# A scratch round trip in a planned stream of instructions: the read back as a step of its own, and a plan that no longer counts the turning

## The chip, the core and the metric

The kernel runs on one core of a Trainium2 chip. The core has five engines that each work through their own list of instructions in order: TensorE (PE, with its weight loads shown as PEld), VectorE (DVE), ScalarE (ACT), GpSimd (POOL) and SyncE (SP). SP issues nearly all DMAs of this kernel, and since its list is in order too, an issue that waits holds back all that stand behind it. The engines wait for each other through semaphores. The metric is the device time of one execution in microseconds; the number that counts is the median of several runs.

## What is computed

One inference step of a trunk of two layers over 512 prompt tokens and 32 sample tokens, with 1024 features. Layer 0 mixes tokens with RWKV-7 time mixing, layer 1 with differential attention; both also attend to a memory of 256 tokens, gate the result and project it back:

```
def rwkv_layer(x, mk, mv, prev_row, S0, ...):
    h = rmsnorm(x, norm_w)
    p, qm, gate = split(h @ w_in)
    y_mix, S_T, last_row = rwkv_mixer(p, prev_row, S0, ...)
    y_mem = mem_attention(qm, mk, mv)
    out = concatenate([y_mix, y_mem]) * silu(gate)
    return x + out @ w_out, S_T, last_row

def step(S, inp):                      # inside rwkv_mixer, for every token and each of 24 heads
    r_t, k_t, v_t, w_t, kk_t, a_t = inp
    sa = einsum('bhvk,bhk->bhv', S, -kk_t)
    S = S * w_t + sa * (kk_t * a_t) + v_t * k_t
    return S, einsum('bhvk,bhk->bhv', S, r_t)
```

Everything is in float32. The change is in layer 0.

## The kernel before

**Blocks.** The projections `h @ w_in` go block by block: one block is 128 columns of the weight, that is 1024 x 128 numbers. They are loaded as two halves (tile `raw`, `load`, L264, five buffers). Each half is split for TensorE into a rounded part `whi` (a cast on ScalarE) and the rest `wlo` (a subtraction on VectorE) (`split`, L293), and a block then takes 48 products into two PSUM tiles `ps_g` (`steps`, L348). In layer 0 these products are the filling between all else, and the list of TensorE is laid out so that it always has some.

**Pairs.** The 24 heads are done as 12 pairs. The recurrence over tokens is cut into chunks of 64. A pair's *preparation* (`rw_prep`, L645) makes decays, keys and the small matrices of each chunk; it is a Python generator, and each `yield` ends a step. It has 33 steps. Near its end it needs the keys turned round, tokens on partitions. VectorE's transpose turns blocks of 32 x 32 only (two instructions from `bk` into `bt`); the blocks themselves are put in their places by a round trip through scratch memory in DRAM:

- step 30: the two transposes, and four DMAs from `bt` to the scratch `tscr`;
- steps 31 and 32: the values are turned on TensorE and copied to `sv`;
- step 33: one DMA of 512 KB from `tscr` back to the whole tile `bt`.

A DMA that reads what another wrote waits, on its issuing queue, until those have landed. `bt` and `tscr` have two buffers each. The pair's *chain* (`chunk`, L957) multiplies by a slice of `bt` in each of its chunks.

**Other steps around it.** A pair's triangular matrices go to scratch (`sc1`, step 26 of the preparation), are inverted on GpSimd (`inv`, L851), and come back in two steps (`back`, L875, and `at`, L885). `val`, `mrg`, `smp`, `out` and `fin` are further generators of a pair. `go(kind, pr)` (L1476) calls the next step of one of them.

**The order.** For layer 0 the order on every engine and queue is the order in which the program issues (`tie`, L123). First come three lists: `FILL0`, `FILL1` and `FILL2` (L83 on) call a step of the preparation of pair 0, 1 and 2, each followed by so many products of the blocks (loops at L1587, L1595, L1610). After that each pair's chain runs in 23 steps, numbered from 0, by `PLAN` (L49). Each step has two halves, and each half lists what is called there: a kind, the distance of its pair from the pair of the chain, its cost on TensorE's side and its cost on VectorE, both in us. The products are handed out so that TensorE's costs are spread evenly. Products, casts and subtractions all come from one stream (L1557), which asks for the load of a block two blocks ahead.

**Work put off.** The casts and subtractions of the next block, and some other evacuations, are put off into a queue (`put_off`, L305). Each half step calls `some(room)` (L315), with

```
room = (sum(load) + 2.3 * each[pr] / 48) / len(PLAN)
spent += self.some(room * (k + (half + 1) / 2) + 0.4 - spent)
```

where `load` holds the VectorE costs of the steps, `each` the products of the pair, and `spent` what VectorE has been booked for so far in the pair. A subtraction has the cost `LATER` (0.75) and is issued only when the allowance is at least that; casts cost nothing and go at once. What is still in the queue when its block begins is issued there (`until`, L310).

**The end of pair 9.** Pairs are numbered from 0. When the chain of pair 9 is through (`pr + 3 == NPAIR`), the last steps of the preparation of pair 11 are called, with the 24 products that were kept back (`KEPT`). Then its pool of tiles is closed, and the pool of the memory attention takes its place. That attention begins with loads of the cached memory keys (`cmt` and others, `mem_steps`, L1242), at step 0 of the next pair, and turns them on TensorE (`ps_ck`) at step 2.

Of the kernel before, what the change touches and what calls it, by code (L numbers as in the profile page):

```python
# [46 lines left out]
LATER = 0.75  # L47
FULL = ("full", 0, 0, 0)
PLAN = [  # L49
    [[("val", 0, 0.95, 0), ("prep", 2, 0.1, 0)], [("prep", 2, 0, 0), ("prep", 1, 0, 1.42)]],  # L50
    [[("prep", 2, 0, 1.04)], [("prep", 1, 0.53, 0)]],
    [[], [("prep", 1, 0, 0), ("prep", 2, 0.56, 1.0)]],
    [[("prep", 2, 0, 0)], [("prep", 2, 0, 1.0)]],
    [[("smp", 0, 0.11, 0.28)], [("prep", 2, 0, 0.86)]],
    [[("out", -1, 0.11, 0)], [("prep", 2, 0, 0.84)]],
    [[("prep", 2, 0, 1.1), ("smp", 0, 0.21, 0.29)], [("prep", 2, 0, 0.86)]],
    [[("prep", 2, 1.1, 1.37)], [("smp", 0, 0.21, 0), ("prep", 1, 0, 0)]],
    [[], [("prep", 2, 0, 0.9), ("prep", 2, 1.1, 1.37)]],
    [[], []],
    [[("smp", 0, 0.6, 0.85)], [("prep", 2, 0.5, 0.58)]],  # L60
# [13 lines left out]
SHIFTED, ASKED, KEPT = 13, 19, 24  # L74
# [34 lines left out]
class Trunk:  # L109
# [535 lines left out]
    def rw_prep(self, st, rkv):  # L645

        nc, p, pr = self.nc, self.rp, st["pr"]
        yield
        k = rkv["k"]()
# [177 lines left out]
        yield  # L827
        scr = self.dp.tile([2 * TP, P], F32, tag="tscr", name="tscr", bufs=2)
        tb = self.rb.tile([P, 8, P], F32, tag="bt", name="bt", bufs=2)
        bt[:2] = tb[:, :4], tb[:, 4:]  # L830
        for q in range(2):
            self.ve.transpose(bt[q].rearrange("p j c -> p (j c)"), bk[:, q * TP : q * TP + TP])
        to = scr[:].rearrange("(b i) (a c) -> a i b c", i=TS, c=TS)
# [8 lines left out]
        for u in range(2):  # L842
# [2 lines left out]
            sv[u] = self.rb.tile([P, 4, P], F32, tag="sv", name="sv", bufs=4)  # L845
            self.ae.copy(sv[u][:64, 0:4:2, :], pv[:64, 2 * u : 2 * u + 2])
            self.ae.copy(sv[u][64:, 1:4:2, :], pv[64:, 2 * u : 2 * u + 2])
        yield
        self.se.dma_start(tb[:], scr[:].rearrange("(j p) c -> p j c", p=P))

    def rw_invert(self, st):  # L851
# [593 lines left out]
    def layer0(self, mem):  # L1445
# [6 lines left out]
        with ExitStack() as ctx:  # L1452
# [18 lines left out]
            sts = [{"pr": pr} for pr in range(NPAIR)]  # L1471
# [4 lines left out]
            def go(kind, pr):  # L1476

                if kind == "rsq":
                    self.rsqrt(self.r20[:], self.q20[:], self.rk0, "nt")
                elif 0 <= pr < NPAIR:  # L1480
                    if kind in ("inv", "back", "at"):
                        {"inv": self.rw_invert, "back": self.rw_back, "at": self.rw_at}[kind](sts[pr])
                        return
                    if (kind, pr) not in run:
                        it = run[kind, pr] = self.rw_prep(sts[pr], rkv[pr]) if kind == "prep" else make[kind](sts[pr])
                        next(it)
                    next(run[kind, pr], None)
# [90 lines left out]
            def fill(n, each=6):  # L1578

                while n > 0:  # L1580
                    for _ in range(min(n, each)):
                        next(main)
                    n -= each
                    self.some(LATER)

            self.ordered = True
            for k, n in enumerate(FILL0):  # L1587
                go("prep", 0)
                if k == 3:
                    go("rsq", 0)  # L1590
                    self.split_roots()
                if k == 26:
                    go("inv", 0)
                fill(n)
            for k, n in enumerate(FILL1):  # L1595
                go("prep", 1)
                if k == 3:
                    go("rsq", 1)
                    self.split_roots()
                fill(n)  # L1600
            self.mctx.close()
            self.rb2 = self.pool("rwb2", 1, ctx=rctx)
# [22 lines left out]
            for pr in range(NPAIR):  # L1625
                mplan = MPLAN.get(pr, ())
                kept = KEPT if pr + 3 == NPAIR else 0
                took = [HOP + sum(us for x in y for kind, d, us, _ in x if 0 <= pr + d < NPAIR) for y in PLAN]
                load = [HOPV[k % 3] + sum(us for x in y for kind, d, _, us in x if 0 <= pr + d < NPAIR) for k, y in enumerate(PLAN)]
                whole = sum(took) + MEMPE * len(mplan) / 12 + MAIN * (each[pr] - kept)  # L1630

                pace = [max(x, 1.4) for x in load] if each[pr] < 3 * 6 * KT else [1.0] * len(PLAN)
                due = [whole * sum(pace[:k]) / sum(pace) for k in range(len(PLAN) + 1)]
                room = (sum(load) + 2.3 * each[pr] / 48) / len(PLAN)
                t, left, spent = 0.0, each[pr] - kept, 0.0
                for k, y in enumerate(PLAN):
                    go("chain", pr)
                    t += HOP
                    spent += HOPV[k % 3]
                    for half, x in enumerate(y):  # L1640
                        for kind, d, us, vus in x:
                            if kind == "prep" and pr == 0 and d == 2 and ready:
                                ready -= 1
                            elif 0 <= pr + d < NPAIR and kind != "full":
                                go(kind, pr + d)
                                t += us
                                spent += vus
                        for at, h in mplan:
                            if at == k + half / 2:
                                if h not in mit:  # L1650
                                    mit[h] = self.mem_steps(mems[h], 0, h, self.ma, 2)
                                    next(mit[h])
                                next(mit[h], None)
                                t += MEMPE / 12
                        if half and pr == LAM and k in (1, 7):
                            (self.lam_in if k == 1 else self.lam_out)()
                        if half and pr + 1 < NPAIR and k == ASKED:
                            self.state_in(pr + 1)
                        if half and pr == NPAIR - 2 and k == SHIFTED:
                            self.shift_out()  # L1660
                        if half and pr == NPAIR - 2 and k % 2 and len(came) < EARLY:
                            came.append(self.fetch(early, OUT_ORDER[len(came)]))
                        if half and k in SPLIT.get(pr, ()):
                            self.put_split(came[len(made)])
                            made[OUT_ORDER[len(made)]] = came[len(made)][:2]
                        if FULL not in x:
                            spent += self.some(room * (k + (half + 1) / 2) + 0.4 - spent)
                        while left and t + MAIN / 2 < (due[k + 1] if half else (due[k] + due[k + 1]) / 2):
                            next(main)
                            t += MAIN  # L1670
                            left -= 1
                while left:
                    next(main)
                    left -= 1
                if pr + 3 == NPAIR:
                    for _ in range(4):
                        go("prep", pr + 2)
                        fill(KEPT // 4)
                    while self.later:
                        self.later.pop(0)[0]()  # L1680
                    ca.close()
                    early = self.pool("wo0e", 1, ctx=mctx, side="right")
                    self.ma = self.pool("mem0a", 1, ctx=ma, side="right")
# [10 lines left out]
        with ExitStack() as ctx:  # L1694
# [63 lines left out]
            pr = [self.psc.tile([P, 512], F32, tag="c", name="ps_r") for _ in range(2)]  # L1758
# [557 lines left out]
```

## Time and profile before

| what | value |
|---|---|
| median of 3 runs (lowest to highest) | 1368.79 us (1366.13 to 1370.41) |
| time of the profiled execution | 1368.89 us |
| its span, first to last instruction | 1366.9 us |
| TensorE busy | 1318.2 us, 96% |
| VectorE busy | 964.0 us, 71% |
| ScalarE busy | 806.7 us, 59% |
| GpSimd busy | 356.9 us, 26% |
| mean granted TensorE clock | 0.992 |
| layer 0's twelve chains (first and last product with `bt`) | 141.5 to 677.5 us |
| writes to `tscr`, issues | 48 of 128 KB, 86.7 to 576.1 us |
| reads from `tscr`, issues | 12 of 512 KB, 94.0 to 579.8 us |

Times in rows are microseconds from the start of the span. A row of the timeline has the start, the duration, the engine, the line, the operation, output and inputs by the names in the program, and how many instructions are merged in it; in brackets stands the idle time of the engine before it and what ended that. A duration on SP is that of the issue alone, not of the transfer. A row of the waits says which engine waited with which tile for whom, the total, how many times, and the longest. PE's busy time includes pipelined ends. Line 106 is a helper through which nearly all instructions of the kernel are issued, so the names of tiles tell them apart.

### The profile page before, as it was taken

The numbers are of one execution on the slowest core, as the hardware profiler recorded it, in microseconds if no ns is written. First come the engines' busy times: TensorE is split into PE (matmuls) and PEld (weight loads), VectorE is DVE, ScalarE is ACT, GpSimd is POOL, SyncE is SP. The second block draws the span as 40 slices with busy tenths as digits, with TensorE's granted clock in tenths as the row PEclk, the third lists the DMA queues.
The fourth block names the chain that finished last, engine by engine and source line by source line (L and its number), as shares of the span: only waits on it lengthen the run. The fifth ranks groups of instructions, "written<-read, shape, count | busy, mean of one in ns | idle before, by whom it ended". The sixth has DMA issues, their size and how long they took to land. (4 is left out here: it accounts for less than half of the span.)

```text
span 1366.9 us, 31492 instructions
## 1 busy us (share of the span) xinstructions
PE 1318.2 (96%) x11566; PEld 1259.5 (92%) x11566; DVE 964.0 (71%) x2367; ACT 806.7 (59%) x2270; POOL 356.9 (26%) x833
## 2 busy tenths in 40 slices
PE   8989999999999999889999999999999999999997
PEld 6978899999998999888899999999999999999997
DVE  5766778888888888646774487876488757887443
ACT  5755678767776777546543366664467546674222
POOL 2136678556765577610000000000000001002000
PEclk9999999999999999999999999999999999999999
DMA  6463444444443444352275565662266533763322
GB/s 222 145 149 79 104 101 101 87 105 116 100 99 101 108 99 110 78 163 86 65 209 134 136 186 142 152 153 82 86 147 159 126 89 91 172 148 96 93 78 74
DMA packets 433204, 163.04 MB, mean 119 GB/s; under 512 B 213289, under 2 KB 423602, under 8 KB 433050
## 3 DMA queue, kind: packets, MB, share of 16 engines
q1 hardware_dynamic: 432986, 161.02, 46.3%
q8 instruction: 91, 1.49, 0.5%
q14 instruction: 63, 0.52, 0.1%
q10 hardware_dynamic: 64, 0.02, 0.0%
HBM read 124.29 MB, written 36.48 MB: 118 GB/s over the span
## 5 line engine op out<-in xcount | busy, mean ns | idle before, releaser
L106 PE MATMUL ps_g<-hh,wlo 128*128 128x272 f32 x1808 | 540.7, 300 | 6.9 <-DVE wlo L106 6.7
L106 PE MATMUL ps_g<-hl,whi 128*128 128x272 f32 x1808 | 537.0, 298 | 0.9 <-DVE hl L106 0.7
L106 PE MATMUL ps_g<-hh,whi 128*128 128x272 f32 x1808 | 531.0, 295 | 1.2 <-DVE ats L106 0.8
L106 PEld LDWEIGHTS ps_g<-hh,wlo 128*128 128x128 f32 x1808 | 342.6, 190 | 10.8 <-DVE wlo L106 9.3
L106 PEld LDWEIGHTS ps_g<-hh,whi 128*128 128x128 f32 x1808 | 343.2, 190 | 4.9 <-DVE ats L106 1.0
L106 PEld LDWEIGHTS ps_g<-hl,whi 128*128 128x128 f32 x1808 | 342.4, 190 | 5.0 <-DVE hl L106 1.8
L106 DVE TENSOR_TENSOR wlo<-raw,whi 128x512 fp32r<-128x512 f32 x314 | 215.2, 698 | 111.6 <-ACT whi L106 109.4
L106 ACT CAST whi<-raw 128x512 fp32r<-128x512 f32 x314 | 188.9, 619 | 120.8 <-PE ps_g L106 60.2
L871 POOL TENSOR_TENSOR tm<-u,m 102x84 f32<-102x84 f32 (+23 forms) x341 | 143.6, 421 | 115.5 <-DMA m<-sc 68.5
L873 POOL TENSOR_TENSOR u<-u,tm 102x84 f32<-102x84 f32 (+23 forms) x341 | 145.0, 425 | 26.7
L106 PE MATMUL ps_g<-hi,wlo 128*128 128x272 f32 x512 | 147.7, 288 | 1.4 <-DVE wlo L106 1.4
L106 PE MATMUL ps_g<-hi,whi 128*128 128x272 f32 x512 | 147.8, 289 | 0.2 <-ACT whi L106 0.2
L106 PE MATMUL ps_g<-lo,whi 128*128 128x272 f32 x512 | 147.4, 288 | 0.0
L1344 POOL TENSOR_TENSOR lo<-og,hi 128x544 fp32r<-128x544 f32 x8 | 13.2, 1652 | 377.1 <-ACT hi L106 376.6
L106 PEld LDWEIGHTS ps_g<-hi,wlo 128*128 128x128 f32 x512 | 96.4, 188 | 1.8 <-DVE wlo L106 1.8
L106 PEld LDWEIGHTS ps_g<-hi,whi 128*128 128x128 f32 x512 | 96.6, 189 | 0.4 <-ACT whi L106 0.4
L106 PEld LDWEIGHTS ps_g<-lo,whi 128*128 128x128 f32 x512 | 96.4, 188 | 0.0
L106 ACT ACTIVATE pt<-ps_s,snm 128x128 f32<-128x128 f32 (+3 forms) x96 | 50.2, 526 | 57.2 <-DVE snm L106 57.2
L106 ACT COPY sv<-ps_c 64x64 f32<-64x64 f32 x192 | 39.4, 205 | 48.8 <-PE ps_c L106 39.8
L106 DVE SCALAR_TENSOR_TENSOR SB<-ps_c,dl,sd 64x64 f32<-64x64 f32 x168 | 47.4, 282 | 22.4 <-PE ps_c L106 18.6
L1811 POOL MEMSET qs<- 128x128 f32 x2 | 0.3, 204 | 198.2 <-PE ps_g L106 198.2
L106 ACT ACTIVATE sg<-ps_g 128x272 f32<-128x272 f32 x64 | 25.1, 393 | 38.0 <-PE ps_g L106 34.0
(394 smaller groups left out, 2496.6 us busy)
## 6 DMA issues: line engine op xcount, KB each, us to landing
raw<-in_rw_in_dram SPq DMA_DIRECT2D x114, 256.0 KB
raw<-in_df_in_dram SPq DMA_DIRECT2D x112, 256.0 KB
raw<-in_w_out_dram SPq DMA_DIRECT2D x64, 256.0 KB
tscr<-bt SPq DMA_DIRECT2D x48, 128.0 KB
bt<-tscr SPq DMA_DIRECT2D x12, 512.0 KB
oscr<-sg SPq DMA_DIRECT2D x16, 272.0 KB
lo<-oscr SPq DMA_DIRECT2D x16, 272.0 KB
m<-sc SPq DMA_DIRECT2D x33, 128.0 KB
```

Source lines behind the costliest of these rows:

```text
L106: return lambda *a, **k: self.trunk.tie(self, issue(*a, **k))
L871: nc.gpsimd.tensor_tensor(tm[:, :n, :wd], u3[:, :n, kx : kx + 1].to_broadcast(sh), m3[:, kx : kx + 1, kx + 1 :].to_broadcast(sh), ALU.mult)
L873: nc.gpsimd.tensor_tensor(u3[:, :n, kx + 1 :], u3[:, :n, kx + 1 :], tm[:, :n, :wd], ALU.add)
L1344: (self.nc.gpsimd if g % 2 and self.o1 else self.ve).tensor_tensor(lo[:], t, hi[:].bitcast(F32), ALU.subtract)
L1811: nc.gpsimd.memset(t[:], 0.0)
```

## The change

The last step of the preparation becomes a function of its own, `rw_get`, and the plan has a kind for it, `get`. In the plan it stands in the second half of step 7, where a step of the preparation stood before. Pair 0 has its read back in the list of `FILL1`, at position 20. The preparation has 32 steps now, so the loop at the end of pair 9 calls three, with 8 products each, instead of four with 6. And in the plan the preparation's step in the second half of step 0 is booked with 0.42 us of VectorE instead of 1.42.

```diff
@@ -47,14 +47,14 @@
 PLAN = [
-    [[("val", 0, 0.95, 0), ("prep", 2, 0.1, 0)], [("prep", 2, 0, 0), ("prep", 1, 0, 1.42)]],
+    [[("val", 0, 0.95, 0), ("prep", 2, 0.1, 0)], [("prep", 2, 0, 0), ("prep", 1, 0, 0.42)]],
     [[("prep", 2, 0, 1.04)], [("prep", 1, 0.53, 0)]],
     [[], [("prep", 1, 0, 0), ("prep", 2, 0.56, 1.0)]],
...
-    [[("prep", 2, 1.1, 1.37)], [("smp", 0, 0.21, 0), ("prep", 1, 0, 0)]],
+    [[("prep", 2, 1.1, 1.37)], [("smp", 0, 0.21, 0), ("get", 1, 0, 0)]],
...
@@ -827,7 +827,7 @@
         tb = self.rb.tile([P, 8, P], F32, tag="bt", name="bt", bufs=2)
-        bt[:2] = tb[:, :4], tb[:, 4:]
+        bt[:2], st["tb"] = (tb[:, :4], tb[:, 4:]), (tb, scr)
@@ -845,7 +845,10 @@
             self.ae.copy(sv[u][64:, 1:4:2, :], pv[64:, 2 * u : 2 * u + 2])
-        yield
+
+    def rw_get(self, st):
+
+        tb, scr = st["tb"]
         self.se.dma_start(tb[:], scr[:].rearrange("(j p) c -> p j c", p=P))
@@ -1478,8 +1481,8 @@
-                    if kind in ("inv", "back", "at"):
-                        {"inv": self.rw_invert, "back": self.rw_back, "at": self.rw_at}[kind](sts[pr])
+                    if kind in ("inv", "back", "at", "get"):
+                        {"inv": self.rw_invert, "back": self.rw_back, "at": self.rw_at, "get": self.rw_get}[kind](sts[pr])
@@ -1597,6 +1600,8 @@
                     go("rsq", 1)
                     self.split_roots()
+                if k == 20:
+                    go("get", 0)
                 fill(n)
@@ -1673,9 +1678,9 @@
                 if pr + 3 == NPAIR:
-                    for _ in range(4):
+                    for _ in range(3):
                         go("prep", pr + 2)
-                        fill(KEPT // 4)
+                        fill(KEPT // 3)
                     while self.later:
                         self.later.pop(0)[0]()
                     ca.close()
```

## The prediction

> **What bounds the kernel now.** I read the page first, then the stretches, then who waits for whom on PE, then the DMA queue of SyncE (SP).
>
> ```profile
> span 1366.9 us, 31492 instructions
> PE 1318.2 (96%) x11566; PEld 1259.5 (92%) x11566; DVE 964.0 (71%) x2367; ACT 806.7 (59%) x2270; POOL 356.9 (26%) x833
> ```
>
> The profiled execution took 1368.9 us with a span of 1366.9, and the median of the runs is 1368.8, so a difference in the span is one in the time. PE is busy nearly everywhere; what can be won is its idle time, and the time in which its clock is halved. The stretches (length, then busy time of PE, PEld, DVE, ACT, POOL, then granted clock, DMA share, GB/s):
>
> ```profile
> 86.71:90.06 3.35, 2.10 (x24) 1.72 (x23) 0.57 (x2) 2.77 (x7) 0.00 (x0) 1.00 0.89 182
> 90.06:92.40 2.34, 2.34 (x22) 2.33 (x20) 1.96 (x8) 1.48 (x6) 1.88 (x6) 1.00 0.92 132
> 92.40:95.00 2.60, 2.60 (x20) 2.30 (x19) 1.58 (x7) 1.72 (x6) 2.14 (x6) 1.00 0.04 6
> 95.00:99.20 4.20, 3.08 (x25) 2.86 (x23) 0.00 (x0) 0.00 (x0) 3.38 (x11) 1.00 0.97 259
> 103.87:108.60 4.73, 4.73 (x21) 4.73 (x22) 2.43 (x5) 1.84 (x6) 4.03 (x10) 0.50 0.46 133
> 200.00:550.00 350.00, 340.63 (x3615) 320.40 (x3614) 291.22 (x699) 260.27 (x769) 228.60 (x512) 1.00 0.44 104
> 549.00:552.40 3.40, 1.48 (x10) 1.32 (x11) 3.35 (x8) 1.86 (x6) 1.64 (x3) 1.00 0.28 42
> 552.40:555.80 3.40, 3.40 (x16) 3.28 (x16) 1.86 (x5) 0.39 (x2) 0.02 (x1) 0.50 0.36 59
> 574.44:579.20 4.76, 4.46 (x55) 4.08 (x53) 1.20 (x4) 2.70 (x8) 3.90 (x12) 1.00 0.75 110
> 579.20:580.50 1.30, 0.00 (x0) 0.00 (x0) 0.69 (x2) 0.00 (x0) 1.13 (x3) 1.00 0.01 1
> 580.50:584.26 3.76, 0.00 (x1) 0.03 (x1) 0.00 (x0) 0.00 (x0) 2.95 (x10) 0.85 0.91 261
> 584.26:589.90 5.64, 5.64 (x22) 5.28 (x23) 0.32 (x1) 2.36 (x7) 1.66 (x7) 0.50 0.63 204
> 690.00:1366.90 676.90, 666.26 (x5254) 653.23 (x5252) 444.83 (x1117) 343.63 (x942) 15.89 (x16) 1.00 0.50 128
> ```
>
> From 690 us on PE is busy for 666 of 677 us, so what layer 0 saves, the end comes earlier by. In layer 0 there are three stretches at half clock. PE's waits from 84 to 600 us (total, times, longest):
>
> ```profile
> PE ps_g L106 <- DVE wlo L106: 6.5, 9, 0.7
> PE ps_b L106 <- ACT r L106: 5.8, 1, 5.8
> PE ps_ck L106 <- DMA cmt<-in_cache_mem_k_dram: 5.4, 1, 5.4
> ```
>
> Two single waits of 5.8 and 5.4 us, and a small one that comes back nine times. What lies ahead of the first, on SP and on ScalarE, and PE itself:
>
> ```profile
> 86.71 3.35 SPq L106 DMA_DIRECT2D tscr<-bt  x4
> 94.02 0.38 SPq L106 DMA_DIRECT2D bt<-tscr  x1
> 94.49 0.64 SPq L106 DMA_DIRECT2D raw<-in_rw_in_dram  x1
> ```
> ```profile
> 99.20 0.62 ACT L106 CAST whi<-raw 128x512 fp32r<-128x512 f32 x1 [4.95 <-DMA raw<-in_rw_in_dram]
> ```
> ```profile
> 103.87 1.25 PE L106 MATMUL ps_b<-r,hs 128*128 128x128 f32 x5 [5.79 <-ACT r L106]
> ```
>
> SP has issued the four writes of the turned keys by 90.06 and then stands still until 94.02: the read back waits for the writes to land, and the weight load is queued behind it. The load goes out at 94.49, its cast starts at 99.20 after ScalarE had idled 4.95, and PE idles 5.79 behind that. The second place, at the end of pair 9, has the same form:
>
> ```profile
> 574.44 2.69 SPq L106 DMA_DIRECT2D tscr<-bt  x4
> 579.83 0.38 SPq L106 DMA_DIRECT2D bt<-tscr  x1
> 580.25 0.57 SPq L106 DMA_DIRECT2D cmt<-in_cache_mem_k_dram  x1
> ```
> ```profile
> 584.26 0.66 PE L106 MATMUL ps_ck<-ident,cmt 128*128 128x128 f32 x2 [5.36 <-DMA cmt<-in_cache_mem_k_dram]
> ```
>
> And SP's own waits on these writes:
>
> ```profile
> SPq L106 <- DMA tscr<-bt: 6.4, 3, 3.8
> ```
>
> Three of twelve read backs wait at all, and nearly all of it is 3.8 us at 94.02 and 2.6 at 579.83. The other nine come long after their writes.
>
> **Part 1: the read backs move.** Counting the steps of a preparation (33 before, 32 after), pairs 2 to 10 had their 33rd step in step 7 of the plan, second half, which is just where "get" stands now (pairs and plan steps are numbered from 0): for them nothing moves. Pair 0's read goes from the end of its own preparation to step 20 of pair 1's, pair 1's from plan step 2 to 7 (there was hardly a wait to win), pair 11's from the end of pair 9 to step 7 of the next chain. Each is one instruction of 0.38 us on SP; at its new place it stands among weight loads that are asked for two blocks ahead, and its tile is read only in the chain of its pair.
>
> *First gap.* With the read gone, the load follows the writes at 90.06 instead of 94.49. Its buffer is the one that the subtraction five half blocks back has freed, by my count before the writes went out, so I see no other wait. The DMA engines are at 0.92 until 92.40 with the writes and at 0.04 from there to 95.00. So the load's 256 KB move right after 92.40 (about 1.0 us at the 259 GB/s of 95.00 to 99.20), and with the 0.6 us that lie between the end of the second writes (579.20) and the read they released (579.83), plus some stragglers, the cast can start at 94.7. The bounds are 94.25, where ScalarE is free, and 96. I take 94.7: 4.5 us of the 5.79 go and 1.3 are left. The Trainium skill, page "DMA: Bandwidth & Descriptors", section "Queues, rings and completion order", says that a DMA engine takes descriptors in ring order; that speaks against a larger gain, since a load issued behind the writes cannot overtake them. No row here shows the order inside a ring; a load served beside the writes would give up to 0.45 us more here and 1.2 more at the second gap.
>
> Then the clock. From 103.87 to 108.60 PE ran at 0.50, so 2.4 of these 4.73 us are lost work. The rows show when the clock falls: 1.25 us idle of 3.35 (86.71 to 90.06) left it at 1.00, 1.92 idle of 3.40 (549.00 to 552.40) halved it. A rest of 1.3 is next to the first, so I count the 2.4 as won; if not, it stays. The Trainium skill, page "TensorE: Matmul & The Clock Gate", section "Part 1: The HAM clock gate (the "warmup" mystery)", has the clock fall after an idle window of about 3.4 us; the trace differs, 1.92 us of idle in such a window did it. By that rule the half clock of 552.40 to 555.80 would not be there.
>
> What is late next: VectorE, which has its own chain from there to the first products of the pair.
>
> ```profile
> 112.27 1.06 DVE L106 TENSOR_TENSOR bk<-rkv,cum 128x512 f32<-128x512 f32 x2
> ```
> ```profile
> 113.83 1.16 PE L106 MATMUL ps_at<-zr,bk 64*128 64x128 f32 x16
> ```
>
> `bk` is ready 0.5 us before PE takes it. PE would come 4.5 + 2.4 = 6.9 earlier, VectorE 4.5 plus about 1.2 of the idle time it has there while the slow PE finishes a block; 6.9 - 5.7 - 0.5 = 0.7 is given back. First gap: 4.5 + 2.4 - 0.7 = **6.2 us** (bounds 2.0 and 7.5).
>
> *Second gap.* The load of `cmt` goes out at 577.2 instead of 580.25, behind writes that keep the DMA engines busy to 579.20. Its 128 KB take 0.5 us at 261 GB/s, and 0.6 to landing: 580.3. PE has been there since 578.90, so it waits 1.4 instead of 5.36: 3.9 won. The half clock from 584.26 to 589.90 costs 2.8, won with the same reason. That the last preparation now runs as three steps with 8 products each instead of four with 6 leaves the same 24 products. Second gap: **6.7 us** (bounds 2.0, if only the read's transfer ahead of it goes, and 8.1).
>
> **Part 2: the plan's VectorE account.** The turning still costs VectorE what it did:
>
> ```profile
> 311.35 1.30 DVE L106 STREAM_TRANSPOSE bt<-bk 128x512 f32<-128x512 f32 x2
> ```
>
> Only the account changes: a pair's sum of VectorE costs in the plan falls from 32.52 to 31.52, the allowance per step from (32.52 + 4 x 2.3) / 23 = 1.814 to 1.770, and what is booked after step 0 is 1.0 less. A subtraction that was put off is issued when the allowance is at least 0.75. At step 8, first half, it was 8.5 x 1.814 + 0.4 - 15.64 = 0.18; now it is 8.5 x 1.770 + 0.4 - 14.64 = 0.81. So in pairs 1 to 8 the first subtraction of the gate's next block moves from step 11 to step 8, and the second from the last moment before that block to step 11. Where they stood (VectorE, then PE):
>
> ```profile
> 283.69 1.29 DVE L106 TENSOR_TENSOR at<-ps_at,mk 128x512 f32<-128x512 f32 x2 [1.25 <-PE ps_at L106]
> ...
> 287.67 1.29 DVE L106 TENSOR_TENSOR wlo<-raw,whi 128x512 fp32r<-128x512 f32 x2
> ```
> ```profile
> 199.41 0.40 PE L106 MATMUL ps_g<-hh,wlo 128*128 128x272 f32 x1 [0.73 <-DVE wlo L106]
> ...
> 288.42 0.39 PE L106 MATMUL ps_g<-hh,wlo 128*128 128x272 f32 x1 [0.73 <-DVE wlo L106]
> ...
> 510.88 0.39 PE L106 MATMUL ps_g<-hh,wlo 128*128 128x272 f32 x1 [0.73 <-DVE wlo L106]
> ```
>
> PE waits 0.73 us for them in each of these eight pairs, from 199.41 to 510.88. At step 8 VectorE idles 1.25 just before 283.69, so the first (half of 1.29) costs nothing there; if that cover were gone it would push 0.65 into the pair's chain. Of the nine waits on `wlo` eight are these: 8 x 0.73 = **5.8 us** won. Later in the pair two other subtractions come one or two places later, still two steps before their block. VectorE is busy 291 of 350 us, so some other wait can appear; I give back 1.0 for all pairs (bounds 0 and 5.8).
>
> *Pair 9 (it has fewer products to cover with).* One subtraction leaves the stretch 549.00 to 552.40, where VectorE is busy 3.35 of 3.40, and joins a full stretch at step 3. That moves up to 0.7 us of waiting forward, and may lift the half clock of 552.40 to 555.80 (1.7 us). I take 0.5 won (bounds -0.7 and 2.2).
>
> Sum: 6.2 + 6.7 + 5.8 - 1.0 + 0.5 = 18.2 us; 1368.9 - 18.2 = 1350.7.
>
> **Rivals.**
>
> *The loads have waits of their own.* SP waits 181.7 us for subtractions over the run:
>
> ```profile
> SPq L106 <- DVE wlo L106: 181.7, 79, 9.3
> ```
>
> A wait on several things is put down to the last, so the load at 94.49 may have had one that ended at 94, and `cmt`, whose pool opens where the preparation's closed, one near 579. Then only the read's transfer goes: 512 KB at 260 GB/s, 2.0 us at each place, and both half clocks stay: 2.0 + 2.0 + 5.8 - 1.0 + 0.5 = 9.3, 1359.6 us. Against it: my count of the buffers. By the clock rule of "TensorE: Matmul & The Clock Gate" in the Trainium skill the second rest of 3.4 us (5.36 - 2.0) could just keep the clock, which would make this rival 1356.8.
>
> *The regrouping brings nothing:* PE finds the next wait where it was 0.73 ahead. Then 6.2 + 6.7 = 12.9, 1356.0.
>
> *The moves don't do what they say:* something else holds both gaps, and only the plan counts: 5.8 + 0.5 - 1.0 = 5.3, 1363.6. Against it: the read is the very row ahead of both late loads.
>
> *A later limit takes the gain*, such as the inversions on GpSimd ahead of the first chain: within 4 us of before.
>
> *Slower.* The two subtractions at steps 8 and 11 push the chain's adds behind them, 1.3 us a pair instead of 0.73, and with the small idle times beside it PE's idle passes 1.9 us in 3.4: the clock halves for a stretch in every pair, 1.7 us. It costs 8 x (0.6 + 1.7) = 18.4 instead of winning 5.8, against 12.9 won at the gaps: 1374.4. It decides from where the idle time before 283.69 is under 0.65; it is 1.25, which speaks against it.
>
> **Numbers.** Forecast 0.62, its own range 1344 to 1356. Loads with waits of their own 0.14, no use of the regrouping 0.09, moves without effect 0.06, a later limit 0.04, slower 0.05. About 0.3% or 4.1 us is what a measurement of this kernel can tell from no change: under 1364.7 counts as faster. The first four cases lie there: 0.91, less 0.02 for the edge of the fourth, is faster 0.89; the later limit and that edge are same 0.06; slower is 0.05. The range goes from 1343 (gap bounds, the half clock of pair 9 gone, and 1.5 for the spread of runs) to 1363, which takes in the first two rivals and most of the third.
>
> **What would show it.** Right: no wait of SP on `tscr`; the loads of 94.49 and 580.25 out 3 to 4 us earlier against the writes; PE's two waits at 1 to 1.5 us; no stretch at half clock after them; the eight waits of 0.7 on `wlo` gone. Wrong: SP still idle between writes and load under another name; a half clock after a rest of 1.4; new waits of PE on `avz` or `SB` in each pair near step 8.

## The result, and the profile after

| | median | lowest to highest | ratio to before, 95% interval |
|---|---|---|---|
| before | 1368.44 us | 1366.13 to 1370.41, 4 runs | |
| after | 1347.55 us | 1345.98 to 1347.91, 4 runs | 0.9846 (0.9828 to 0.9863) |

The changed kernel is faster by 21 us, 3 more than forecast and inside the range. Of all executions in this document one is left out of the numbers, of `pair0_back` below, which took 2240 us at a granted clock of 0.71. The profiled execution of the changed kernel took 1347.47 us. From the page after:

```profile
span 1345.5 us, 31479 instructions
PE 1312.6 (98%) x11566; PEld 1258.0 (93%) x11566; DVE 965.2 (72%) x2367; ACT 806.6 (60%) x2270; POOL 363.2 (27%) x833
```

VectorE's work is the same 965 us. TensorE's count of instructions is the same too, and its share rose from 96 to 98%: what went is waiting, and some of the time at half clock, which counts as busy (TensorE's busy time fell by 5.6 us). SyncE's queue at the end of pair 0's preparation, after:

```profile
87.11 3.27 SPq L106 DMA_DIRECT2D tscr<-bt  x4
90.48 1.98 SPq L106 DMA_DIRECT2D raw<-in_rw_in_dram  x2
...
100.03 0.50 SPq L106 DMA_DIRECT2D bt<-tscr  x1
```

The weight loads follow the writes at once, and the read back stands ten microseconds later, where its data have long landed: SyncE has no wait on `tscr` left. At the end of pair 9 it is the same:

```profile
558.28 2.69 SPq L106 DMA_DIRECT2D tscr<-bt  x4
561.01 0.86 SPq L106 DMA_DIRECT2D cmt<-in_cache_mem_k_dram  x1
```

TensorE's longest waits from 84 to 600 us, after (total, times, longest):

```profile
PE ps_ck L106 <- DMA cmt<-in_cache_mem_k_dram: 1.7, 1, 1.7
PE ps_w L106 <- DVE t1b L106: 1.6, 2, 1.0
...
PE ps_b L106 <- ACT r L106: 0.9, 1, 0.9
...
PE ps_g L106 <- DVE wlo L106: 0.6, 1, 0.6
```

The wait of 5.8 is 0.9, that of 5.4 is 1.7, and of the nine waits on `wlo` one is left (0.6). One line is new near the top: `ps_w` on `t1b`, the first products with pair 0's inverted matrices, 1.6 us in two waits. Before, TensorE waited there too, 0.62 and 0.61 us. Behind these waits there is a new half clock. Two stretches after (length, busy time of PE, PEld, DVE, ACT, POOL, granted clock, DMA share, GB/s):

```profile
126.98:130.39 3.41, 1.77 (x43) 1.40 (x42) 1.53 (x3) 1.53 (x6) 2.85 (x8) 1.00 0.46 94
130.40:133.80 3.40, 3.40 (x43) 3.07 (x42) 0.69 (x1) 2.17 (x6) 2.80 (x8) 0.50 0.57 162
```

It lasts 10.24 us, to 140.6, and it is the only one left in layer 0: the three of before, at 101.8, 552.4 and 583.1 us, are gone.

**Where the time went.** The same products have a start in both traces, and the difference of these starts says how much was won by then in these two executions:

| product | before | after | won by then | so this stretch |
|---|---|---|---|---|
| first `ps_at` of pair 1 | 113.84 | 107.16 | 6.67 | +6.7 (first gap) |
| first product of chain 0 with `bt` | 141.50 | 138.03 | 3.47 | -3.2 (new half clock) |
| of chain 1 | 179.38 | 175.75 | 3.63 | +0.2 |
| of chain 9 | 534.30 | 519.16 | 15.13 | +11.5 (pairs 1 to 8) |
| of chain 10 | 577.04 | 560.87 | 16.17 | +1.0 (pair 9) |
| of chain 11 | 634.47 | 612.34 | 22.13 | +6.0 (second gap) |
| end of the execution | | | 21.4 | -0.7 |

### The profile page after: what moved, and what is told of

Same layout as the page of the kernel before. It is cut to its first block, busy times and chain, and to the rows that moved or that the text cites. A ratio compares the mean times of both kernels' runs of the same rounds, so it can differ in the third digit from the quotient of the medians.

```text
span 1345.5 us, 31479 instructions
## 1 busy us (share of the span) xinstructions
PE 1312.6 (98%) x11566; PEld 1258.0 (93%) x11566; DVE 965.2 (72%) x2367; ACT 806.6 (60%) x2270; POOL 363.2 (27%) x833
## 5 line engine op out<-in xcount | busy, mean ns | idle before, releaser
L876 POOL TENSOR_TENSOR u<-u,tm 102x84 f32<-102x84 f32 (+23 forms) x341 | 149.3, 438 | 26.7
```

The source lines that it names most:

```text
L876: nc.gpsimd.tensor_tensor(u3[:, :n, kx + 1 :], u3[:, :n, kx + 1 :], tm[:, :n, :wd], ALU.add)
```

## The experiments

The theory: three independent gains, the two gaps (SyncE stands for the landing of the writes, with a load behind it) and the plan's account. The rivals: only the 512 KB of the read ahead of the loads cost something; the account alone, or the moves alone, do it all. And a new question: what makes the half clock before the first chain? The first four kernels ran on one chip, where the kernel before took 1367.87 us (median of 11).

**Undo one part at a time.** Pair 0's read back at its old place:

```diff
+                if k == 32:
+                    go("get", 0)
...
-                if k == 20:
-                    go("get", 0)
```

> The changed kernel (1347.5 us), with the read back of pair 0 alone put at the end of its own preparation again. Theory of the wait: SP stands still behind the four writes, the weight load goes out some 4 us later, PE idles over 5 us before ps_b and runs at half clock after it: slower by 4 to 7 us, 1351.5 to 1354.5. Rival, loads with waits of their own: only the read's transfer comes back, about 2 us, 1349.5. Rival, the place of this read has no effect: 1347.5. Open beside these: the changed kernel has a new stretch at half clock from 130 to 141 us; if it comes of the phase of the clock windows it may be gone here, and the difference be smaller by up to 3 us.

Measured: 1352.41 us, the median of five runs (1351.31 to 1353.94); ratio 0.9877 (0.9848 to 0.9906). SyncE and TensorE:

```profile
93.86 0.38 SPq L106 DMA_DIRECT2D bt<-tscr  x1
94.34 1.08 SPq L106 DMA_DIRECT2D raw<-in_rw_in_dram  x2
```
```profile
103.67 1.25 PE L106 MATMUL ps_b<-r,hs 128*128 128x128 f32 x5 [5.58 <-ACT r L106]
```

The gap is back at 5.58, with its half clock from 101.2 to 108.1. So the read back's place alone makes the first gap. The half clock before the first chain is not there (the waits before `ps_w` are 0.65 and 0.83). That the one comes in exchange for the other does not hold: `before_042` and `wait_alone` below have both.

Pair 11's read back at the end of pair 9:

```diff
                         fill(KEPT // 3)
+                    go("get", pr + 2)
```

> The changed kernel, with the read back of pair 11 alone put at the end of pair 9 again. Theory of the wait: cmt goes out 3 us later, PE idles over 5 us before ps_ck and then runs at half clock: slower by 5.5 to 7 us, 1353 to 1354.5. Rival, loads with waits of their own: about 2 us, 1349.5. Rival, no effect: 1347.5.

Measured: 1350.81 us (1347.85 to 1355.48), ratio 0.9864 (0.9833 to 0.9894).

```profile
569.51 0.66 PE L106 MATMUL ps_ck<-ident,cmt 128*128 128x128 f32 x2 [5.33 <-DMA cmt<-in_cache_mem_k_dram]
```

The second gap is back with 6.8 us at half clock behind it. The trace is of an execution of 1355.48 us. By their times alone this kernel and `pair0_back` can hardly be told from the changed one (0.9846, 0.9828 to 0.9863), and this one came out faster than its expectation; it is the rows that show what came back.

The old account, with all moves:

```diff
-("prep", 1, 0, 0.42)
+("prep", 1, 0, 1.42)
```

> The changed kernel, with the plan's VectorE cost of the turning at 1.42 again and the read backs as changed. As forecast: eight waits of 0.73 us on wlo come back, slower by 5 to 6 us, 1353. As the two traces read now (a pair takes 1.4 us less, of which about 1.0 at the wait on wlo and 0.4 at ps_y): slower by 11 to 12 us, 1359. Rival, the regrouping has no use: 1347.5.

Measured: 1355.69 us (1354.92 to 1359.09), ratio 0.9904 (0.9877 to 0.9932). The row of its waits:

```profile
PE ps_g L106 <- DVE wlo L106: 6.5, 9, 0.7
```

All nine are back. From chain 0 to chain 9 this kernel wins 0.1 us on the kernel before, where the changed one wins 11.7: the whole of that stretch is the account's. The time lies between the two that were expected: this run kept its clock before the first chain, which starts 3.2 us earlier than in the changed kernel.

The account alone, in the kernel before:

```diff
-("prep", 1, 0, 1.42)
+("prep", 1, 0, 0.42)
```

> The kernel before (1368.4 us), with the plan's cost at 0.42 alone. As the traces read: faster by 11 to 12.5 us, 1357, with the waits of 5.8 and 5.4 us and the half clock behind them still there. As forecast: faster by 5 to 6, 1363. Rival, the account does nothing by itself: 1368.4.

Measured: 1360.27 us (1358.59 to 1361.18), ratio 0.9932 (0.9905 to 0.9959). Both big gaps are there (5.4 and 5.3), the eight waits on `wlo` are gone, and the new half clock before the first chain is there as well:

```profile
133.87:137.28 3.41, 1.76 (x40) 1.41 (x39) 1.53 (x3) 1.42 (x4) 2.80 (x8) 1.00 0.31 51
137.29:140.69 3.40, 3.40 (x45) 2.97 (x46) 0.70 (x1) 2.30 (x6) 2.77 (x9) 0.50 0.65 187
```

From chain 0 to chain 9 this kernel wins 11.4 us, but chain 0 starts 3.8 us later than before, so its time too lies between the two that were expected.

The half clock does not need the moves, then, but the account does not make it either. Up to the first products of chain 0 the kernel before and this one issue the same instructions in the same order on every engine and on SyncE, and so do the changed kernel and `plan_142`. In each of these two pairs one profiled run kept its clock and the other lost it. Nor does it come of TensorE being there earlier: `plan_142` comes to `ps_w` first of the four (127.64), waits 0.60 and 0.55 us and keeps its clock, this kernel comes last (135.70), waits 0.98 and 0.67 and loses it. The window of `plan_142` with both waits:

```profile
125.55:128.96 3.41, 2.25 (x44) 1.95 (x43) 1.47 (x3) 1.56 (x6) 2.78 (x9) 1.00 0.28 44
```

What makes these waits longer in one run than in another stays open. None of the parts does it all; the rivals that said so fall.

**What of the gap is waiting, and what is bytes.** The changed kernel with a read of one row of the scratch at the two old places: it waits as the read back did and moves 512 bytes.

```diff
+    def peek(self, st):
+        one = self.dp.tile([1, P], F32, tag="peek", name="peek", bufs=2)
+        self.se.dma_start(one[:], st["tb"][1][:1, :])
```

> The changed kernel, with a read of one row of the scratch (512 bytes, touched by all four writes) issued at the two places where the read backs of pairs 0 and 11 used to stand; the real reads stay at their new places. So SyncE waits there as before, without the 512 KB. My theory: wait and bytes add up, 2.7 of the 4.7 us that PE idled more before ps_b are the standing of SyncE and 2.0 the transfer ahead of the load. Then PE's wait before ps_b is 3.6 (0.89 in the changed kernel, 5.58 with the read back in its old place), the one before ps_ck 3.3, both long enough to halve the clock, and the time some 5 over the changed kernel, 1352 to 1353. Rival, the bytes do it all: both waits stay under 2.0, the clock stays whole, 1347 to 1349. Rival, the wait does it all: 5.6 and 5.3, 1354 to 1356.

This kernel, the next one, `fill_24` and `mem_late` ran on a chip where the kernel before took 1369.97 us (median of 9). Measured: 1354.84 us (1353.02 to 1356.25), ratio 0.9888 (0.9863 to 0.9914).

```profile
93.80 0.56 SPq L106 DMA_DIRECT2D peek<-tscr  x1
94.45 1.21 SPq L106 DMA_DIRECT2D raw<-in_rw_in_dram  x2
```
```profile
102.50 1.25 PE L106 MATMUL ps_b<-r,hs 128*128 128x128 f32 x5 [4.47 <-ACT r L106]
```

And with 512 KB copied from the input to a spare place in DRAM, which waits for nothing:

```diff
+    def peek(self, st):
+        copy = self.dp.tile([2 * TP, P], F32, tag="peek", name="peek", bufs=2)
+        self.se.dma_start(copy[:].rearrange("(j p) c -> p j c", p=P),
+                          self.a["x_prompt"][0, :P, :].rearrange("p (j c) -> p j c", c=P))
```

> The changed kernel, with an unrelated transfer of 512 KB (128 rows of the input, in pieces of 512 bytes, to a spare place in DRAM) issued at the two old places, which waits for nothing. My theory: PE's wait before ps_b is 0.89 + 2.0 = 2.9, the one before ps_ck 1.72 + 2.0 = 3.7, both halve the clock, and the time is 4 to 6 over the changed kernel, 1352 to 1353. Rival, the bytes do it all: 5.6 and 5.3, 1354 to 1356. Rival, the wait does it all: both waits stay as in the changed kernel within 0.5, and the time within 1 of it, 1347 to 1348.5.

Measured: 1353.24 us (1350.80 to 1354.73), ratio 0.9876 (0.9850 to 0.9902).

```profile
101.77 0.73 PE L106 MATMUL ps_b<-r,hs 128*128 128x128 f32 x5 [3.44 <-ACT r L106]
```

| PE's wait | after | wait alone | bytes alone | both (read back in its old place) |
|---|---|---|---|---|
| before `ps_b` | 0.89 | 4.47 | 3.44 | 5.58 |
| before `ps_ck` | 1.72 | 3.94 | 4.12 | 5.33 |

Both cost, each more than I had expected, and they do not add up: 3.6 + 2.6 against 4.7 at the first place, 2.2 + 2.4 against 3.6 at the second. SyncE's standing is the larger half at the first place; at the second they are even. Each alone was enough to halve the clock at both places. The copy between two places in DRAM is not the read back itself, so its share is the less certain one.

**Cover the new wait.** If 8 products more stood ahead of `ps_w`, they would cover its first wait:

```diff
-FILL3 = [16, 0, 2, 6]
+FILL3 = [24, 0, 2, 6]
```

> The changed kernel, with 24 instead of 16 products laid ahead of the first products of the first chain, ps_w (8 fewer are left for that chain). My theory: the new half clock from 130 to 140 us comes from PE's two waits there, 1.01 and 0.62 us, on the return of the inverted matrices. 8 products of 0.125 us cover the first one; the half clock goes, which is worth about 3 beside the 1.0: 1343 to 1344.5. Rival, the half clock there has another cause than these waits: 1346.5 and a half clock still there. Rival, the 8 products are missed by the first chain, whose waits grow by as much: no change, 1347 to 1348.

Measured: 1350.29 us (1349.08 to 1352.77), ratio 0.9860 (0.9838 to 0.9882): nothing won. PE and ScalarE:

```profile
128.19 0.69 PE L106 MATMUL ps_w<-t1b,at 32*32 32x32 f32 x30 [0.43 <-DVE t1b L106]
131.86 1.06 PE L106 MATMUL ps_w<-at,t1b 32*32 32x32 f32 x32 [1.93 <-ACT t1b L106]
...
166.97 0.24 PE L106 MATMUL ps_w<-t1b,at 32*32 32x32 f32 x2 [1.16 <-DVE t1b L106]
```
```profile
130.43 0.62 ACT L106 CAST whi<-raw 128x512 fp32r<-128x512 f32 x1 [3.08 <-DMA raw<-in_rw_in_dram]
131.07 0.74 ACT L106 COPY t1b<-ps_w 32x256 f32<-32x256 f32 x2
```

The first wait shrank as meant, but the half clock before the first chain stayed (10.24 us). The fourth portion of products let one more piece of put-off work go: a cast, whose load came late, now stood ahead of ScalarE's copy of `t1b`, and TensorE stood 1.93 us for it. And in the chain of pair 0, which has 8 products fewer, waits of about 1 us appeared and halved the clock a second time.

To tell these two causes apart, a later kernel took the 24 products in three portions, so that the cast stays where it was (together with the edit of `mem_late`, below):

```diff
-                fill(n)
+                fill(n, each=8)
```

> mem_late with 24 products ahead of ps_w as in fill_24, but as three portions of 8 instead of four of 6, so that no cast of ScalarE comes to stand ahead of the copies of t1b (there it waited for a load that SyncE had queued behind the returning matrices, and PE 1.93 us behind it). Theory: that cast was what made fill_24 fail; now the wait before ps_w is 0.4, the one of 1.93 is gone, the half clock too, and the time 2 to 3 under mem_late. Rival: the first chain misses the 8 products whatever stands ahead (waits of 0.88, 0.86 and 1.16 there in fill_24): the same as mem_late within 1, or 1 to 2 slower if the clock halves in the chain.

Measured: 1346.65 us (1345.46 to 1348.44), ratio 0.9837 (0.9823 to 0.9852), 3 us over the kernel with that edit alone in the same set. The wait of 1.93 is gone, but in the first chain there are waits of 1.25 and 1.23 and a half clock:

```profile
146.81 1.16 PE L106 MATMUL ps_at<-zr,bk 64*128 64x128 f32 x16 [1.25 <-DVE bk L106]
...
164.68 0.24 PE L106 MATMUL ps_w<-t1b,at 32*32 32x32 f32 x2 [1.23 <-DVE t1b L106]
```

The rival holds: the first chain needs those products. The wait before `ps_w` cannot be filled out of that chain.

**Cover the rest of the second gap.** The first transposes of the memory attention one step later:

```diff
-MPLAN = {10: [(0, 0), (2, 0), (3, 0), (4, 0)
+MPLAN = {10: [(0, 0), (3, 0), (3.5, 0), (4, 0)
```

> The changed kernel, with the first transposes of the memory attention, ps_ck, one step of the plan later in pair 10 (the step after it half a step later). My theory: the 1.72 us that PE still waits before ps_ck are only the landing of cmt, which stands behind the four writes of the turned keys; a step of the plan holds about 1.9 us of work of PE, so the wait is gone or under 0.3 and the time 1.5 shorter, 1346. Rival, the two steps that now follow each other more closely wait for each other (ps_mm on its scores): no change, 1347 to 1348.

Measured: 1343.79 us (1341.71 to 1345.32), ratio 0.9807 (0.9782 to 0.9832). The wait is gone:

```profile
563.48 0.41 PE L106 MATMUL ps_ck<-ident,cmt 128*128 128x128 f32 x2
```

It was measured again, beside the changed kernel, in a third set with `late_24` and `plan_070` (before 1369.92 us there):

> The changed kernel as it is, on the chip of the next three, so that they can be compared with it. 0.985 of the kernel before on the same chip, a half clock before the first chain.

> The same kernel as mem_late, beside the changed one. If its gain of the first time was its own and not the chip's: 2 to 4 us under the changed kernel. If it was the chip's: the same within 1.

Measured: 1345.64 us (1343.59 to 1346.40), ratio 0.9823 (0.9809 to 0.9837), for the changed kernel; 1343.35 us (1341.28 to 1344.56), ratio 0.9807 (0.9792 to 0.9822), with the edit. The intervals overlap a little. The traces speak for a gain of its own: between the starts of chain 10 and chain 11 the two profiles with the edit take 1.7 to 1.9 us less than the two of the changed kernel. It is the fastest version here.

**What the account does.** A value between the two:

```diff
-("prep", 1, 0, 0.42)
+("prep", 1, 0, 0.70)
```

> The changed kernel with 0.70 instead of 0.42 us booked for the keys' step. By the account the first subtraction of the gate's next block then stands at step 9, second half, instead of 8 (11 with 1.42), and the two subtractions late in the pair go back to where they stood with 1.42 (steps 17 and 18, second halves). A pair gained 1.44 us by the change, of which 1.0 at the wait on wlo and 0.4 at that of ps_y on yt. If only the lead of the first subtraction counts, both stay: 0.985 of the kernel before, and 1.4 a pair. If the 0.4 is due to the late subtractions, the wait on wlo stays away and 0.4 a pair is lost: some 3 us over the changed kernel. If step 9 is too late: 0.73 us waits on wlo again, 8 to 11 over.

Measured: 1352.62 us (1350.97 to 1355.92), ratio 0.9879 (0.9863 to 0.9895): 7 us over the changed kernel in that set. None of the three cases as written: the waits on `wlo` stay away, but others come. TensorE from 190 to 600 us:

```profile
PE ps_c L106 <- DVE SB L106: 3.3, 4, 1.2
PE ps_y L106 <- DVE yt L106: 2.1, 7, 0.4
```

VectorE shows where both come from:

```profile
193.40 0.48 DVE L106 TENSOR_TENSOR ats<-ps_ats,mk 128x128 f32<-128x128 f32 x2
193.80 2.03 DVE L106 TENSOR_TENSOR wlo<-raw,whi 128x512 fp32r<-128x512 f32 x1
195.75 0.57 DVE L106 SCALAR_TENSOR_TENSOR SB<-ps_c,dl,sd 64x64 f32<-64x64 f32 x2
...
386.01 0.77 DVE L106 TENSOR_TENSOR wlo<-raw,whi 128x512 fp32r<-128x512 f32 x1
386.71 0.94 DVE L106 TENSOR_TENSOR yt<-yt,q 128x640 f32<-128x640 f32 x1
```

At step 9 the subtraction stands straight ahead of the chain's `SB`, for which TensorE waits 1.22 us behind the row of 2.03. Late in the pair another one stands ahead of `yt`. In the changed kernel, with 0.42, the first lies at step 8 between two `at`, with idle time left behind it, and the late one behind `yt`:

```profile
275.66 0.67 DVE L106 TENSOR_TENSOR wlo<-raw,whi 128x512 fp32r<-128x512 f32 x1
276.99 1.29 DVE L106 TENSOR_TENSOR at<-ps_at,mk 128x512 f32<-128x512 f32 x2 [0.65 <-PE ps_at L106]
...
294.98 0.83 DVE L106 TENSOR_TENSOR yt<-yt,q 128x640 f32<-128x640 f32 x1
295.73 0.81 DVE L106 TENSOR_TENSOR wlo<-raw,whi 128x512 fp32r<-128x512 f32 x1
```

The same work, one and a half steps apart: one place is free, the other costs over half of what the move wins. From chain 1 to chain 9 `plan_070` wins 4.9 us on the kernel before, the changed one 11.5.

## Why the prediction was right, and where it was wrong

**The first gap, right (6.2 forecast, 6.7 measured).** The load went out behind the writes, 0.89 us of waiting were left (1.3 forecast) and the half clock behind it went. That the cast started at 94.68, where 94.7 was forecast, is luck. ScalarE, after:

```profile
93.92 0.75 ACT L106 ACTIVATE cum<-th 128x512 f32<-128x512 f32 x2
94.68 0.62 ACT L106 CAST whi<-raw 128x512 fp32r<-128x512 f32 x1
```

The cast followed ScalarE's own work without idle time, so the load was no longer the limit. That is the early bound of the forecast, 94.25, as the trace after runs 0.4 us later (its writes start at 87.11, not 86.71). The stretch from 86.71 to 90.06, from which the prediction read that 1.25 us of idle time leave the clock whole, lies across two of the windows in which the clock changes (see the last section); with 0.89 us left, this did not matter. `pair0_back` shows that the read's place is the cause, `wait_alone` that SyncE's standing by itself makes 3.6 of the 4.7 us.

**The second gap, right in kind (6.7 forecast, 6.0 measured).** 1.72 us were left where 1.4 were forecast. That the clock stayed whole behind them is in part luck: in `pair0_back` and `plan_142` 1.94 and 1.86 us were left, and the clock halved for 3.4 us. Not the 0.2 us make the difference but the windows in which the clock is judged (see the last section). In the changed kernel the wait falls into two of them, in `pair0_back` into one:

```profile
560.48:563.89 3.41, 2.23 (x18) 2.04 (x17) 1.45 (x4) 1.56 (x3) 2.94 (x7) 1.00 0.92 163
563.90:567.30 3.40, 2.86 (x21) 2.79 (x22) 0.00 (x0) 1.99 (x7) 2.70 (x9) 1.00 0.77 223
```
```profile
565.44:568.85 3.41, 1.48 (x13) 1.31 (x12) 0.88 (x2) 0.39 (x3) 2.86 (x8) 1.00 0.88 198
```

**The loads with waits of their own, wrong as a rival.** It held that only the read's transfer goes. The loads went out at once, and `wait_alone` makes a gap of 4.47 with no transfer.

**The plan's account, the mis-sized term (5.8 - 1.0 forecast, 11.5 measured).** Two things were missing. First, the idle time in a row understates a stall. Products of TensorE ahead of and behind the wait at 199.41, before:

```profile
198.26 0.29 PE L106 MATMUL ps_g<-hh,whi 128*128 128x272 f32 x1
198.39 0.29 PE L106 MATMUL ps_g<-hl,whi 128*128 128x272 f32 x1
...
199.64 0.29 PE L106 MATMUL ps_g<-hh,whi 128*128 128x272 f32 x1
199.77 0.29 PE L106 MATMUL ps_g<-hl,whi 128*128 128x272 f32 x1
```

A product shows 0.29 us but the next starts after 0.13. From 198.39 two steps to 199.64 took 1.25 instead of 0.26, so the wait shown as 0.73 was worth 1.0: 8.0 for the eight. Second, the two late subtractions, for which I gave 1.0 back as a risk, were a gain: one used to stand ahead of `yt`, and `ps_y` waited up to 0.4 us a pair for it. VectorE, before:

```profile
302.41 0.68 DVE L106 TENSOR_TENSOR wlo<-raw,whi 128x512 fp32r<-128x512 f32 x1
303.01 0.94 DVE L106 TENSOR_TENSOR yt<-yt,q 128x640 f32<-128x640 f32 x1
```

`plan_070`, in which one stands there again, has seven such waits. The stretch gives 11.5 / 8 = 1.44 a pair. Laid side by side product by product, the two traces put 1.0 of it at the wait on `wlo` (what is won grows from 4.90 to 5.91 us in one pair and from 6.67 to 7.67 in the next) and the rest around `ps_y` (0.8 and 0.4 in these two pairs).

**The price of the slower case was real, its place was not.** That a subtraction ahead of the chain's adds costs TensorE more than a wait on `wlo` is just what `plan_070` shows at step 9 (1.22 us against 0.73, with the subtraction itself held up, see the last section). At step 8 the idle time of VectorE that the prediction pointed to covered it.

**Pair 9 (0.5 forecast, 1.0 measured), right by luck.** The half clock from 552.4 to 555.8 went, which lay within the bounds, but not by the account: it is gone in `plan_142` as well, which has the old account. From chain 9 to chain 10 the kernel before takes 42.75 us, `plan_142` 40.89 and the changed kernel 41.70. So the stretch is 1.9 us shorter without the half clock, and the account cost 0.8 of that, about the 0.7 of waiting that the prediction's lower bound has.

**A later limit, left out of the sum.** The prediction gave the later limit 0.04 and let it take nearly all or nothing. In the profiled execution it took 3.2 us: TensorE waited 1.63 us in all before `ps_w` for the returning matrices, where it had waited 1.23, and the clock halved for 10 us. It is not shown that the change made this wait longer: `plan_142`, with both moves, waits 1.15 there, and `before_042`, with none, 1.65. What the prediction had not looked at is how near the clock was to falling there already:

```profile
132.56:135.97 3.41, 2.19 (x44) 1.89 (x42) 1.46 (x3) 1.44 (x5) 2.85 (x8) 1.00 0.29 46
```

That is the kernel before: 2.19 us busy of 3.41, at full clock. After it was 1.77. The account's term, too small by 6.7, and this one, left out, partly cancelled. That the sum of 18.2 came nearer to 21.4 than its parts is luck.

## What to carry to other kernels

A read back of data that was just written belongs well behind its write, here ten microseconds: not for the sake of the read but of whatever stands behind it on the issuing queue, here a weight load. When costs in a planner only set the order of filling work, judge a change of them by where each piece lands against the chain's own instructions, since a step later can cost over half of what the move wins. And look at the places where the same engine idles for a microsecond or two: ask how near each is to a half clock, and compare several traces there before a half clock is put down to a change.

## What the runs showed of the hardware

**The clock changes on a fixed grid.** In the records of the clock, the stretches between two changes are 92.16, 6.83, 443.73, 3.41, 27.31 and 6.83 us before, 119.47, 10.24 and 1201.49 after: all multiples of 3.413 us. The grid's place against the program differs from run to run. The Trainium skill, page "TensorE: Matmul & The Clock Gate", section "Part 1: The HAM clock gate (the "warmup" mystery)", has this free-running window of 3413 ns, and the trace agrees. But it has the clock fall after an idle window, and here a window that was more than half busy is enough. Counted on each run's own grid, PE's busy time in a window that ended in a fall or just escaped it, and the number of products in it:

| window (run) | PE busy of 3.41 us | products | the clock then |
|---|---|---|---|
| before, 548.98 | 1.47 | 10 | falls |
| after, 126.98 | 1.77 | 43 | falls |
| `plan_142`, 541.98 | 1.88 | 14 | stays |
| `pair0_back`, 131.95 | 1.93 | 18 | stays |
| `wait_alone`, 131.85 | 2.03 | 43 | falls |
| `bytes_alone`, 129.98 | 2.06 | 43 | stays |
| `mem_late_again`, 126.08 | 2.07 | 46 | falls |
| before, 132.56 | 2.19 | 44 | stays |

The border lies near 2 us, about 60%, and is not sharp in busy time. Part of that is what the products are. In all 14 traces, a window at full clock with no product of 32 x 32 in it was followed by a fall up to 1.55 us busy, and by none from 1.89 on; with 32 such products it was followed by a fall up to 2.07 in all but one case, and by none above. In `late_24` the clock fell after a window of 2.83, with 77 products in it, 64 of them of 32 x 32:

```profile
128.14:131.55 3.41, 2.83 (x77) 2.42 (x77) 1.10 (x2) 1.43 (x4) 2.86 (x8) 1.00 0.67 181
131.56:134.97 3.41, 3.41 (x36) 3.04 (x34) 0.84 (x1) 1.61 (x6) 2.86 (x8) 0.50 0.62 179
```

That small products count for less is my reading; no run changed their size alone. At the second gap the grid explains why a wait of 1.7 to 1.9 us halves the clock in one run and not in another: it depends on whether it falls within one window. Before `ps_w` it does not, since there both waits lie in one window in all twelve traces with this order; what differs is their sum, 1.15 to 1.69 us, and how many of the small products share the window with them.

**VectorE and GpSimd shut each other out.** The subtraction of 2.03 us in `plan_070` takes 0.67 elsewhere. Beside it, GpSimd:

```profile
193.93 1.35 POOL L792 TENSOR_TENSOR rkk<-rkv 128x544 f32<-128x544 f32 x1
```

0.67 + 1.35 = 2.02. (The instruction of GpSimd ahead of it, from 193.75, was still running when the subtraction began.) The Trainium skill, page "SBUF — State Buffer", section "SBUF: two separate sides", has the two engines share a pair of ports as an exclusive lock, which one holds for a whole instruction while the other blocks, if VectorE reads two operands from SBUF as this one does. The trace agrees: the sum, not a part of it. Two more subtractions in that run take 1.42 and 1.63 us; each began while the same product of GpSimd, 1.36 and 1.35 us long, had 0.9 and 1.1 us to go, so they too come near the sum.
